# One transformer-style layer on one core: bias tables, masks, attention stacks and the program's head moved to other places

## The chip, the core and the metric

The kernel runs on one core of a Trainium2 chip. The metric is device microseconds of one execution, of which the median over several runs is taken. A profile of one execution comes with it. Engine names are those of the profile: PE is TensorE (PEld its weight loads), DVE is VectorE, ACT is ScalarE, POOL is GpSimd, SP is SyncE, which here only issues transfers.

## The reference

One layer over x of 1024 tokens by 1024 features, float32, with a norm before and after each of three parts:

```
h = swiglu(rmsnorm(x, g)) ; x = x + 0.5 * rmsnorm(h, g')           # FFN 1, width 2816
q, k, v = rmsnorm(x, g) @ w_qkv                                     # 16 heads of 64
o_na  = neighbourhood attention of heads 0-7 on a 16 x 64 grid of tokens,
        window 8 x 16, with a learned bias per (row, column) offset
o_dil = heads 8-15: windows (128,1), (512,4), (2048,16), T5 bias, merged by softmax weights
x = x + rmsnorm([norm(o_na) | norm(o_dil)] @ w_out, g)
h = swiglu(rmsnorm(x, g)) ; x = x + 0.5 * rmsnorm(h, g')           # FFN 2
```

## The kernel before

Every float32 product is three matmuls of split operands (`mm3`: hi*hi, hi*lo, lo*hi); ACT makes the high part with a cast and DVE the low part with a subtraction. The FFNs and the value and q/k projections run as products of halves in a Strassen-like scheme of seven passes per 2 x 2 blocks (`PASSES`).

The program is a chain of stages. PE's order is written by hand throughout (`ordered`); in the first lines of the program that of DVE and ACT too. Elsewhere a planner orders the other engines by its own costs; `c.behind(f, ENGINE)` puts what `f` issues behind the last instruction that the engine was given so far, and `queued` does so for SP and POOL, whose queues issue the transfers. `plan(n, {turn: [...]})` and `c.todo` hang side work on turns of a stage, one turn at each `c.tick()`.

1. The head (`begin` in `layer`): x is loaded, the first norm is computed with a square root on ACT (`rstd_by_sqrt`), the gain's row is spread over the partitions by a matmul (`spread_gain`, tile `gps`), the first three gate weights are split.
2. FFN 1. `PairGemm.ahead` makes two of the seven gate and up products for the first nine column blocks; `PairGemm.run` makes the rest in 22 turns ("gated products"); `Passes.run` then multiplies by the down weights ("down stage"). Sums of down weights (`RightSums`) ride on turns of the gated products, those of value weights on turns of the down stage.
3. Values and q/k: two value passes (`vp.run(0, 1)`), the early half of q/k (`pg.ahead`), value passes 2 to 6, then `pg.run`. Value passes take weights from rotating tiles `pw` (pool `pr`) and raw ones `praw` (pool `pw`).
4. Beside value passes 4 and 5 `build_bias` makes two kinds of tables in DRAM: `gab`, for each dilated head 128 rows that each hold the same 511 numbers shifted by one (two transfers, one per dilation), and `nb`, for each neighbourhood head a 128 x 384 table that is first filled with -1e30 and then gets 16 groups of rows from `stk`. All are issued on POOL's queue.
5. Attention, a head at a time, dilated pairs first. `load_head` loads a stack `st` (q twice and both parts of k twice, 128 x 3 x 1024) in four transfers on POOL's queue, values (`va`, `vb` or `vs`) and the bias on SP's. POOL reorders q and bias of the next dilated head, or adds the mask `cmask` to the next neighbourhood bias (line 1557). Results `ob` of the strided part are brought into token order as `obn` by 16 transfers on SP (`regroup`), merged by POOL's two products and DVE's addition (`merge`), and normed (`GroupNorm`). `nat_fillers` makes matmuls of the output projection that `c.fill` puts between units of neighbourhood heads.
6. The output projection, then FFN 2 like FFN 1.

Of the kernel before, what the change touches and what calls it, by code (L numbers as in the profile page):

```python
# [10 lines left out]
F32 = mybir.dt.float32  # L11
# [231 lines left out]
def rstd_by_sqrt(c, ss):  # L243

    nc, k = c.nc, ss.shape[1]
    h, y, e = [c.small.tile([P, 4], F32, tag=t, name=t)[:, :k] for t in ("v", "y", "e")]
    nc.vector.tensor_add(h, ss[:, :, 0], ss[:, :, 1])
    nc.vector.tensor_scalar(h, h, 1.0 / D, EPS, op0=ALU.mult, op1=ALU.add)
    nc.scalar.activation(e, h, AF.Sqrt)
    nc.vector.reciprocal(y, e)  # L250
    nc.vector.tensor_mul(e, y, h)
    nc.vector.tensor_mul(e, e, y)
    nc.vector.tensor_scalar(e, e, -0.5, 1.5, op0=ALU.mult, op1=ALU.add)
    nc.vector.tensor_mul(y, e, y)
    return y


def spread_gain(c, g, tag, row, one):
# [4 lines left out]
    nc.gpsimd.dma_start(row, g)  # L263
# [44 lines left out]
def nat_fillers(c, x, part, halves):  # L308


    for g in halves:
        ws = []
        for t in range(4):
            acc = []
            for k in range(4):
                def filler(g=g, t=t, k=k, ws=ws, acc=acc):
                    ws.extend(() if ws else nat_weights(c))
                    acc.extend(() if acc else [nat_bank(c)])
                    nat_mm(c, acc[0], x, t, k, ws, True, True)
                    if k == 3:  # L320
                        c.nc.scalar.copy(part[:, t, g * T:(g + 1) * T], acc[0])
# [31 lines left out]
class PairGemm:  # L353
# [4 lines left out]
    def __init__(self, c, op, srcs, early, sink):  # L358
        self.c, self.op, self.srcs, self.early, self.sink = c, op, srcs, early, sink
        self.n, self.raw, self.w, self.kept = len(srcs), {}, {}, {}  # L360
# [242 lines left out]
class Passes:  # L603
# [4 lines left out]
    def __init__(self, c, n, left, right, take, last=None):  # L608
# [4 lines left out]
        if self.own:  # L613
            self.groups[0] = [groups[0][:2], groups[0][2:]] + groups[1:]
# [3 lines left out]
    def fetch(self, w=None, raws=()):  # L618
# [4 lines left out]
        if w is None:  # L623
            w = c.pr.tile([P, 1 + self.own, 2, 2, T], F32R, tag="w", name="pw")
            w = [w[:, side] for side in range(1 + self.own)]
        for side in range(1 + self.own):
# [6 lines left out]
            hi, lo = [w[side][:, h, :m] for h in range(2)]  # L633
            nc.scalar.copy(hi, raw[:, :m])  # L634
            nc.vector.tensor_sub(lo, raw[:, :m], hi.bitcast(F32))  # L635
        for j, i in enumerate(ids):
            lhs = [w[0][:, h, j, :] for h in range(2)] if self.own else [h[:, i, :] for h in self.left.x[a]]
            self.ready.append((lhs, [w[-1][:, h, j, :] for h in range(2)]))
# [134 lines left out]
def build_bias(c, rel, t5, onehot, lncount):  # L773
# [4 lines left out]
    t5t = c.bp.tile([32, 8], F32, tag="b0", name="t5t")  # L778
    nc.gpsimd.dma_start(t5t, t5.rearrange("h b -> b h"))
    for i in range(2):  # L780
        oh = c.bp.tile([P, T], F32, tag="oh", name="oh")
        cols = slice(511 * i, 511 * i + 511)
        nc.gpsimd.dma_start(oh[:32, :511], onehot[:, cols])
        lc = c.bp.tile([P, T], F32, tag="lc", name="lc")
        nc.gpsimd.dma_start(lc[:8, :511], lncount[:, cols].broadcast_to([8, 511]))
        ps = c.pst.tile([P, 4, P], F32, tag="tr", name="tabp").rearrange("p a b -> p (a b)")
        nc.tensor.matmul(ps[:8, :511], t5t, oh[:32, :511], start=True, stop=True)
        nc.vector.tensor_add(lc[:8, :511], ps[:8, :511], lc[:8, :511])
        nc.gpsimd.dma_start(tab[i, :, :511], lc[:8, :511])
        g = c.gab[i]  # L790
        dst = bass.AP(tensor=g.tensor, offset=g.offset, ap=[[P * 640, 8], [641, P], [1, 511]])
        nc.gpsimd.dma_start(dst, tab[i, :, :511].unsqueeze(1).broadcast_to([8, P, 511]))
    neg = c.bp.tile([P, T], F32, tag="oh", name="neg")
    nc.gpsimd.memset(neg[:, :384], NEG)
    nc.gpsimd.dma_start(c.nb.rearrange("h p r e -> p h (r e)"), neg[:, :384].unsqueeze(1).broadcast_to([P, 8, 384]))
    for cc in range(8):
        nc.gpsimd.dma_start(stk[cc], rel[:, :, 7 - cc:31 - cc])
    for r in range(16):
        r0 = min(max(r - 4, 0), 8)
        nc.gpsimd.dma_start(c.nb[:, r * 8:r * 8 + 8, r0:r0 + 8, :].rearrange("h c r e -> c h (r e)"),  # L800
                            stk[:, :, r0 - r + 7:r0 - r + 15, :].rearrange("c h r e -> c h (r e)"))

# [52 lines left out]
def load_stack(c, p, hd):  # L855

    nc = c.nc
    st = c.stk.tile([P, 3, SEQ], F32R, tag="st", name="st")
# [38 lines left out]
class DilPair:  # L897
# [78 lines left out]
    def outs(self, hd, part, quad, un, pt, po):  # L976
# [14 lines left out]
        if (hd, part, quad) == (1, 1, 1):  # L991
            self.regroup()
# [4 lines left out]
    def regroup(self):  # L997

        c, nc = self.c, self.c.nc
        self.obn = c.op.tile([P, 8, RW], F32, tag="obn", name="obn")  # L1000
        for ci in range(4):
# [37 lines left out]
def na_v(c, p):  # L1039
    vs = c.vp[0].tile([P, 8, P], F32, tag="v" + "ab"[p % 2], name="vs")  # L1040
    src = c.v[0][:, p * P:(p + 1) * P].rearrange("(r s c) f -> r c s f", r=16, s=8)
    for r in range(16):
        c.nc.sync.dma_start(vs[r * 8:r * 8 + 8], src[r])
# [97 lines left out]
def layer(tc, a, out):  # L1141
    nc = tc.nc
    c = Ctx(tc)
    with ExitStack() as ctx:
# [22 lines left out]
        c.ob = [c.dr.tile([SEQ, RW], F32, name=f"ob{g}") for g in range(4)]  # L1167
# [35 lines left out]
        def one_a_turn(steps, n, first):  # L1203
            plan(n, {first + i: [f] for i, f in enumerate(steps)})

# [10 lines left out]
        def early_pools(stack, n=3):  # L1216
            c.wr, c.sp = pool("wr", 3, stack), pool("sp", n, stack)
# [7 lines left out]
        def ffn(which, op, prep, pg, get, turns, sums, more, post, pre, src, dst, begin=None):  # L1225
# [24 lines left out]
            one_a_turn(sums, NF, NF - 3 - len(sums))  # L1250
            prep2, ps = sub(), []

            def final():
# [9 lines left out]
                ps[0].fetch([w0[:, i] for i in range(2)], raws[:2])  # L1263
                ps[0].fetch([w.rearrange("p (h j) x -> p h j x", h=2) for w in w1], raws[2:])
# [15 lines left out]
            spread(more, 36)  # L1280
# [408 lines left out]
```

## Time and profile before

| | |
|---|---|
| runs | 1956.1 us median of 3 (1954.6 to 1963.72) |
| profiled execution | 1954.35 us |
| its span, first to last instruction | 1952.6 us |
| granted TensorE clock, mean | 0.985 |
| busy: PE, PEld | 1870.2, 1557.4 us |
| busy: DVE, ACT, POOL | 1330.1, 808.5, 327.5 us |
| moved by DMA | 398.11 MB, 204 GB/s over the span |

Matmuls are pipelined, so that busy time of PE is time in which at least one was under way. Idle time of PE in a stage is the window's length less PE's busy time. In a timeline row stand start and length in us, engine, line, operation, what it writes and reads, and in brackets how long the engine sat idle before it and what ended that. A wait for several things is put down to the one that came last by the profile.

### The profile page before, as it was taken

The page shows a single profiled execution, that of the slowest core. Times are in us where ns is not written, and L with a number is a line of the kernel's source. Part 1 is how long each engine was busy: PE and PEld are TensorE (multiplying, and loading weights), DVE is VectorE, ACT ScalarE, POOL GpSimd, SP SyncE. Part 2 cuts the span into 40 slices and gives each one's busy share as a digit, 9 for nine tenths or more (in the row PEclk, how much of TensorE's full clock was granted, in tenths as well). Part 3 has the DMA queues.
Part 4 walks back from the last instruction along what each step waited for, and adds up shares of the span by engine and source line. Part 5 has one row for each costly group of instructions (what it writes and reads, how often), then busy time and mean ns, then how long its engine had stood idle before and what let it go on. Part 6 is the DMA issues. An engine that isn't in the chain of part 4 may idle for free.

```text
span 1952.6 us, 25603 instructions
## 1 busy us (share of the span) xinstructions
PE 1870.2 (96%) x9048; PEld 1557.4 (80%) x9048; DVE 1330.1 (68%) x2234; ACT 808.5 (41%) x1471; POOL 327.5 (17%) x526
## 2 busy tenths in 40 slices
PE   6999999999999999999999788998999999999997
PEld 5788888888888778778898777877888888888886
DVE  6877876775656775477665565676788777755567
ACT  5522333334534554133676555454222333344333
POOL 2101111111000123423434220021011111110000
PEclk9999999999999999999999899999999999999999
DMA  6645566547876668758999981475456665476563
GB/s 228 227 159 192 187 220 225 186 166 268 305 251 204 228 236 281 228 183 242 222 190 157 159 153 49 139 277 189 167 180 202 234 224 190 155 267 219 199 229 138
DMA packets 170322, 398.11 MB, mean 204 GB/s; under 512 B 20097, under 2 KB 41521, under 8 KB 170193
## 3 DMA queue, kind: packets, MB, share of 16 engines
q1 hardware_dynamic: 118800, 222.34, 36.2%
q0 software_dynamic: 50528, 172.03, 27.9%
q10 hardware_dynamic: 864, 2.10, 0.3%
q8 instruction: 71, 1.16, 0.3%
q14 instruction: 59, 0.48, 0.1%
HBM read 272.03 MB, written 127.26 MB: 204 GB/s over the span
## 4 chain that ended last, share of the span: by engine, by line
PE 79%; DMA 7%; DVE 6%; issue 4%; ACT 2%; SPq 1%; POOL 1%; DVEq 0%; POOLq 0%; ACTq 0%
PE mmp L281 16%; PE mmp L283 16%; PE mmp L282 15%; PE accp L281 8%; PE accp L282 8%; PE accp L283 8%; PE po L985 2%; PE ptp L891 1%; PE po L1085 1%; PE trp L159 1%; DMA va<-v 1%; DMA obn<-ob 1%; DMA wraw<-in_wqk_dram 1%; PE sp L965 1%; DMA x<-x 1%
## 5 line engine op out<-in xcount | busy, mean ns | idle before, releaser
L281 PE MATMUL mmp<-x,whi 128*128 128x512 f32 (+1 forms) x1464 | 580.9, 397 | 8.8 <-ACT whi L374 3.5
L283 PE MATMUL mmp<-x,wlo 128*128 128x512 f32 (+1 forms) x1464 | 575.2, 393 | 2.3 <-DVE wlo L375 2.3
L282 PE MATMUL mmp<-x,whi 128*128 128x512 f32 (+1 forms) x1464 | 574.9, 393 | 0.7 <-DVE x L161 0.6
L281 PEld LDWEIGHTS mmp<-x,whi 128*128 128x128 f32 x1464 | 278.3, 190 | 69.0 <-ACT whi L374 4.2
L283 PEld LDWEIGHTS mmp<-x,wlo 128*128 128x128 f32 x1464 | 278.1, 190 | 64.5 <-DVE wlo L375 3.8
L282 PEld LDWEIGHTS mmp<-x,whi 128*128 128x128 f32 x1464 | 278.4, 190 | 59.2 <-DVE x L161 1.5
L635 DVE TENSOR_TENSOR pw<-praw,pw 128x1024 fp32r<-128x1024 f32 (+1 forms) x182 | 199.2, 1138 | 122.8 <-ACT pw L634 122.5
L634 ACT CAST pw<-praw 128x1024 fp32r<-128x1024 f32 (+1 forms) x182 | 169.0, 983 | 208.8 <-PE accp L283 163.8
L374 ACT CAST whi<-wraw 128x1024 fp32r<-128x1024 f32 x129 | 135.1, 1050 | 252.2 <-PE mmp L282 214.5
L281 PE MATMUL accp<-pw 128*128 128x512 f32 x600 | 234.2, 390 | 0.0
L283 PE MATMUL accp<-pw 128*128 128x512 f32 x600 | 233.5, 389 | 0.0
L282 PE MATMUL accp<-pw 128*128 128x512 f32 x600 | 233.4, 389 | 0.0
L375 DVE TENSOR_TENSOR wlo<-wraw,whi 128x1024 fp32r<-128x1024 f32 x129 | 157.6, 1224 | 23.2 <-ACT whi L374 23.0
L283 PEld LDWEIGHTS accp<-pw 128*128 128x128 f32 x600 | 112.6, 188 | 23.7
L282 PEld LDWEIGHTS accp<-pw 128*128 128x128 f32 x600 | 112.7, 188 | 23.3
L281 PEld LDWEIGHTS accp<-pw 128*128 128x128 f32 x600 | 112.6, 188 | 22.8
L581 POOL DMA_DIRECT2D g<-sg x44 | 23.8, 540 | 470.8 <-DVE sg L574 302.7
L535 DVE TENSOR_TENSOR c<-mmp,u 128x512 f32<-128x512 f32 x52 | 35.9, 691 | 83.9 <-PE mmp L283 83.8
L393 ACT COPY s<-mmp 128x512 f32<-128x512 f32 x52 | 30.5, 587 | 145.9 <-PE mmp L283 140.8
L374 ACT CAST whi<-traw 128x512 fp32r<-128x512 f32 x52 | 32.3, 621 | 117.0 <-PE mmp L282 54.8
L462 DVE TENSOR_TENSOR wraw<-wraw 128x1024 f32<-128x1024 f32 x52 | 63.6, 1224 | 23.3 <-DMA wraw<-in_wqk_dram 14.2
L161 DVE TENSOR_TENSOR x<-trp,x 128x512 fp32r<-128x512 f32 x84 | 57.3, 687 | 31.0 <-ACT x L160 30.9
(258 smaller groups left out, 2793.4 us busy)
## 6 DMA issues: line engine op xcount, KB each, us to landing
praw<-g SPq DMA_DIRECT2D x70, 512.0 KB
wraw<-in_wg_dram SPq DMA_DIRECT2D x44, 512.0 KB
wraw<-in_wu_dram SPq DMA_DIRECT2D x44, 512.0 KB
tr<-in_wd_dram SPq DMA_DIRECT2D x44, 512.0 KB
g<-sg POOLq DMA_DIRECT2D x88, 256.0 KB, 3.9
ts<-tr POOLq DMA_DIRECT2D x22, 1024.0 KB, 4.7
praw<-ts SPq DMA_DIRECT2D x88, 256.0 KB
praw<-in_wd_dram SPq DMA_DIRECT2D x66, 256.0 KB
```

Of the source, the lines that this page charges most:

```text
L161: nc.vector.tensor_sub(lo, ps, hi.bitcast(F32))
L281: nc.tensor.matmul(out, ahi, bhi, start=start, stop=False, skip_group_check=go_on)
L282: nc.tensor.matmul(out, ahi, blo, start=False, stop=False, skip_group_check=go_on)
L283: nc.tensor.matmul(out, alo, bhi, start=False, stop=stop, skip_group_check=go_on)
L374: nc.scalar.copy(hi, raw)
L375: nc.vector.tensor_sub(lo, raw, hi.bitcast(F32))
L393: self.c.nc.scalar.copy(s, ps)
L462: nc.vector.tensor_sub(r[:, 0:2], r[:, 1:3], r[:, 0:2])
L535: nc.vector.tensor_add(c21, d, u2)
L634: nc.scalar.copy(hi, raw[:, :m])
L635: nc.vector.tensor_sub(lo, raw[:, :m], hi.bitcast(F32))
L985: nc.tensor.matmul(po[:, un * 2 + j], pt[:, 2 * j + t, :], rhs, start=t == 0, stop=t == 1)
```

## The change

- Tables: `build_bias` becomes `bias_steps`. Its steps are hung on turns 1 to 8 of FFN 1's gated products; each `gab` table is written as four transfers of 32 rows for all eight heads, the fill as two, each step behind the last instruction of POOL.
- Masks: the eight masked neighbourhood tables are made on POOL in the down stage of FFN 1 and stored as `nm`; a head loads both tables from DRAM.
- Stacks: one half (64 partitions) is loaded on POOL's queue and one on SP's; up to head 8 each third stack has a tile of its own, and the loads of a stack and of the rest of a head are separate steps.
- Value slices `vs` of a pair come in 8 transfers of 16 strided partitions instead of 16 of 8; `obn` is fetched in two groups of 8, each after its quad.
- Norms of the dilated half: the steps of the two groups are placed apart, the output projection's weights are fetched earlier, its fillers come as two products each.
- Values and q/k: the first pass starts on two terms; its first tile, and every third early q/k weight, have the pool `p0`; other rotating tiles are one fewer (`pr`, `wr`).
- The head: the gain's row is loaded first, on SP; x tiles 0 and 1 come as halves on SP and ACT; the third weight is fetched at once; the root has one operation less behind it and the order of ACT and DVE is another; one subtraction moves from POOL to DVE.

The diff, cut to its core:

```diff
@@ rstd_by_sqrt, spread_gain
-    nc.vector.tensor_scalar(h, h, 1.0 / D, EPS, op0=ALU.mult, op1=ALU.add)
-    nc.scalar.activation(e, h, AF.Sqrt)
+    nc.vector.tensor_scalar(h, h, 0.5 / D, 0.5 * EPS, op0=ALU.mult, op1=ALU.add)
+    nc.scalar.activation(e, h, AF.Sqrt, scale=2.0)
+    yield
     nc.vector.reciprocal(y, e)
-    nc.vector.tensor_mul(e, y, h)
+    nc.vector.scalar_tensor_tensor(e, y, -1.0, h, op0=ALU.mult, op1=ALU.mult)
     nc.vector.tensor_mul(e, e, y)
-    nc.vector.tensor_scalar(e, e, -0.5, 1.5, op0=ALU.mult, op1=ALU.add)
-    nc.vector.tensor_mul(y, e, y)
+    nc.vector.scalar_tensor_tensor(y, e, 1.5, y, op0=ALU.add, op1=ALU.mult)
...
-    nc.gpsimd.dma_start(row, g)
+    nc.sync.dma_start(row, g)
@@ nat_fillers
-            for k in range(4):
+            for k in (0, 2):
...
-                    nat_mm(c, acc[0], x, t, k, ws, True, True)
-                    if k == 3:
+                    for i in (k, k + 1):
+                        nat_mm(c, acc[0], x, t, i, ws, True, True)
+                    if k:
@@ PairGemm.split_left, Passes.__init__
-            self.w[b] = self.split(self.raw.pop(b), "g")
+            self.w[b] = self.split(self.raw.pop(b), "g", self.own if b % 3 == 0 else None)
...
-        if self.own:
-            self.groups[0] = [groups[0][:2], groups[0][2:]] + groups[1:]
+        self.groups[0] = [groups[0][:2], groups[0][2:]] + groups[1:]
@@ bias_steps (replaces build_bias)
+    def step(turn, f, *args):
+        at.setdefault(turn, []).append(lambda: c.behind(lambda: f(*args), POOL))
...
+    def toeplitz(i, q):
+        g, n = c.gab[i], P // 4
+        dst = bass.AP(tensor=g.tensor, offset=g.offset + q * n * 641, ap=[[641, n], [P * 640, 8], [1, 511]])
+        nc.gpsimd.dma_start(dst, tab[i, :, :511].unsqueeze(0).broadcast_to([n, 8, 511]))
...
+    def masked(h):
+        if h == 0:
+            got["mask"] = c.bp.tile([P, 384], F32, tag="m", name="mask")
+            nc.gpsimd.dma_start(got["mask"], cmask)
+        if h:
+            t = got.pop(h - 1)
+            nc.gpsimd.tensor_add(t, t, got["mask"])
+            nc.gpsimd.dma_start(c.nm[h - 1], t)
+        if h < 8:
+            got[h] = tile("lc" if h % 2 else "oh", 384)
+            nc.gpsimd.dma_start(got[h], c.nb[h].rearrange("p r e -> p (r e)"))
+    for i in range(2):
+        step(2 + 2 * i, load, i)
+        step(4 + 2 * i, table, i)
+        for q in range(4):
+            step(5 + 2 * i + q // 2, toeplitz, i, q)
+    for cc in range(8):
+        step(1 + cc // 4, stack, cc)
+    step(2, clear, 0)
+    step(3, clear, 4)
+    for r in range(16):
+        step(4 + r // 4, rows, r)
+    return at, [lambda h=h: c.behind(lambda: masked(h), POOL) for h in range(9)]
@@ load_stack, regroup, na_v, na_bias
-    for u in range(2):
-        dst = slice(u * 64, u * 64 + 64)
-        nc.gpsimd.dma_start(st[dst, 0, :], q[u, rows, :])
-        nc.gpsimd.dma_start(st[dst, 1:3, :], k[:, rows, :].rearrange("j p n -> p j n"))
+    for u, queue in enumerate((nc.gpsimd, nc.sync)):
+        to = st[u * 64:u * 64 + 64].bitcast(F32)
+        queue.dma_start(to[:, 0, :], q[u, rows, :])
+        queue.dma_start(to[:, 1:3, :], k[:, rows, :].rearrange("j p n -> p j n"))
...
-        if (hd, part, quad) == (1, 1, 1):
-            self.regroup()
+        if hd and part:
+            self.regroup(quad)
...
-    for r in range(16):
-        c.nc.sync.dma_start(vs[r * 8:r * 8 + 8], src[r])
+    for ci in range(8):
+        c.nc.sync.dma_start(vs[ci:P:8], src[ci])
...
+    c.nc.sync.dma_start(nb[:, 1], c.nm[2 * p + hd])
@@ layer: ffn
-            one_a_turn(sums, NF, NF - 3 - len(sums))
+            if tables:
+                c.bp = pool("bp", 1, w)
+            for i, f in enumerate(sums):
+                tables.setdefault(NF - 3 - len(sums) + i, []).append(f)
+            plan(NF, tables)
...
-            spread(more, 36)
+            spread(more + masks, 36)
@@ layer: loading of heads
+                own = i < 9 and i % 3 == 2
+                stacks.append(load_stack(c, *heads[i], c.op if own else c.stk, 1 if own else 2))
...
-        def next_head():
-            if len(loaded) < 2:
-                load_head()
+        def next_head(i):
+            if i != 9:
+                load_st()
+            if i:
+                load_rest()
             return loaded.popleft()
@@ layer: begin (order of the head)
+            op0.gain, *gains = spread_gain(c, a["ffn1_pre_g"], "pre", xn[0][:1], xn[1][:1, :P])
+            for t in range(2):
+                for h, q in enumerate((nc.sync, nc.scalar)):
+                    q.dma_start(xs[t][:, half[h]], x0[t][:, half[h]])
...
+                w2 = c.xp.tile([P, D], F32, tag="xn", name="w2", bufs=c.xn)
+                pg.raw[2] = w2.rearrange("p (i x) -> p i x", i=2)
+                nc.sync.dma_start(w2, pg.srcs[2][0])
...
                 square(0)
+                gains[0]()
                 square(1, 0)
-                square_dve(1, 1)
-                op0.gain, gain0, gain1 = spread_gain(c, a["ffn1_pre_g"], "pre", xn[0][:1], xn[1][:1, :P])
-                gain0()
-                r = [rstd_by_sqrt(c, ss[0])]
+                square(1, 1, xn[1][:, half[1]])
+                root = rstd_by_sqrt(c, ss[0])
+                next(root)
...
                 hi0(0)
-                lo0(0, nc.gpsimd)
-                gain1()
-                scaled(r, 0, 0, 1)
+                gains[1]()
                 square(2)
+                r0 = next(root)
+                scaled(r0, 0, 0, 1)
+                lo0(0)
@@ layer: values and q/k
-            c.pr, c.pw, c.vt = pool("pr", 3, e), pool("pw", 2, e), pool("vt", 2, e)
+            c.pr, c.pw, c.vt = pool("pr", 2, e), pool("pw", 2, e), pool("vt", 2, e)
...
-            plan(8, {0: [lambda: fin.scale(4, 4), A(4, 5)], 4: [U(4)], 5: [lambda: queued(pg.start)]})
+            p0 = pg.own = pool("p0", 1, prep, side="right")
+            vp.fetch([[p0.tile([P, 2, T], F32R, tag="g" + h, name="pw0" + h) for h in ("hi", "lo")]])
+            plan(12, {0: [lambda: fin.scale(4, 4), A(4, 5)], 8: [U(4)], 9: [lambda: queued(pg.start)],
+                      11: [lambda: pg.split_left(0)]})
             vp.run(0, 1, upto=1)
             e.close()
-            early_pools(e, 2)
+            early_pools(e, 2, 2)
...
-            c.behind(lambda: build_bias(c, a["na_rel_bias"], a["t5_rel_bias"], a["onehot"], a["lncount"]), POOL)
@@ layer: attention
-            c.todo.extend([lambda: (queued(c.w.fetch), squares[0]()), squares[1], scales[0],
-                           lambda: (scales[1](), queued(c.w.fetch))]
-                          + puts[:4] + [begin] + puts[4:])
+            c.todo.extend([squares[0], scales[0]] + puts[:4] + [begin, squares[1], lambda: None, scales[1]])
+            for f in puts[4:]:
+                c.todo.extend([lambda: None, f])
...
-            load_head()
...
-                    else:
-                        nc.gpsimd.tensor_add(g[:, 1], g[:, 0], c.cmask)
...
+                    if (p, hd) == (2 * NP - 1, 1):
+                        queued(lambda: [c.w.fetch() for _ in range(2)])
```

More of the change, by code (lines that the diff above doesn't have):

```diff
@@ L1223, in gate_pairs, with ffn @@
             return PairGemm(c, op, [(wg[f], wu[f]) for f in range(NF)], early, GatePairs(c, which))
-        def ffn(which, op, prep, pg, get, turns, sums, more, post, pre, src, dst, begin=None):
+        def ffn(which, op, prep, pg, get, turns, sums, more, post, pre, src, dst, begin=None, tables=()):
             w = sub()
@@ L1402, in begin @@
                 hi1(0)
+                square(3, 0)
+                square(3, 1, junk()[:, half[1]])
+                root = rstd_by_sqrt(c, ss[1])
+                next(root)
                 lo1(0)
-                square(3, 0)
-                square_dve(3, 1)
-                for hi, lo in ((hi0, lo0), (hi1, lo1)):
-                    hi(1)
-                    lo(1, nc.gpsimd)
+                hi0(1)
+                hi1(1)
+                hi2(0)
                 acc, s1 = [pg.bank() for _ in range(3)], []
```

161 lines of the change are left out of this document (85 added, 76 removed).

## The prediction

> **What bounds the kernel now.** I read the page first: the span, the busy table and the chain.
>
> ```profile
> span 1952.6 us, 25603 instructions
> PE 1870.2 (96%) x9048; PEld 1557.4 (80%) x9048; DVE 1330.1 (68%) x2234; ACT 808.5 (41%) x1471; POOL 327.5 (17%) x526
> PE 79%; DMA 7%; DVE 6%; issue 4%; ACT 2%; SPq 1%; POOL 1%; DVEq 0%; POOLq 0%; ACTq 0%
> ```
>
> TensorE is the bound, busy 1870.2 of 1952.6. No matmul of the large products is removed, so a gain can only come from the 82.4 us in which PE is idle and from half-speed clock behind such pauses. Next, therefore, the view by windows, cut at the places of the change (columns: window, length, busy us of PE, PEld, DVE, ACT, POOL, granted clock, DMA share, GB/s).
>
> ```profile
> 0.00:85.00 85.00, 67.96 (x332) 53.88 (x333) 60.26 (x112) 44.66 (x78) 19.90 (x40) 0.98 0.66 229
> 85.00:675.00 590.00, 590.00 (x2602) 485.33 (x2601) 417.46 (x529) 215.77 (x291) 63.72 (x112) 1.00 0.62 218
> 675.00:715.00 40.00, 35.59 (x146) 26.99 (x145) 29.97 (x56) 19.68 (x33) 8.87 (x17) 0.91 0.66 235
> 795.00:845.00 50.00, 44.54 (x181) 35.54 (x180) 19.97 (x27) 6.83 (x8) 18.26 (x31) 0.93 0.72 214
> 935.00:1060.00 125.00, 116.23 (x977) 114.03 (x976) 81.33 (x331) 90.94 (x301) 52.12 (x58) 0.97 0.99 192
> 1085.00:1145.00 60.00, 43.94 (x284) 40.04 (x283) 39.07 (x125) 33.66 (x106) 15.41 (x19) 0.83 0.91 161
> 1145.00:1220.00 75.00, 67.49 (x443) 59.23 (x442) 41.28 (x127) 39.70 (x120) 7.18 (x12) 1.00 0.44 82
> ```
>
> PE idle by stage is length less busy: head 17.0, start of values and q/k 4.4, end of values 5.5, dilated attention 8.8, first neighbourhood heads 16.1, last heads 7.5: 59.3 us, in exactly the stages that the change edits. Clock lost on top is length times (1 - clock): 3.6, 3.5, 3.8 and 10.2 us from the third row on (without 1145, where it is 1.00), at most, since an idle PE loses nothing by it. Between 85 and 675 PE never stops, and two parts of the change go there: they can cost, not gain.
>
> **The change part by part.**
>
> Head. From the timeline:
>
> ```profile
> 5.65 1.06 ACT L151 ACTIVATE junk<-x 128x1024 f32<-128x1024 f32 x1 [2.49 <-DMA x<-in_x_dram]
> 7.88 3.75 PE L268 MATMUL gps<-xn 1*128 1x512 f32 x4 [7.88 <-DMA xn<-in_ffn_pre_g_dram]
> 10.44 0.21 ACT L249 ACTIVATE e<-v 128x2 f32<-128x2 f32 x1
> 11.24 1.26 POOL L1380 TENSOR_TENSOR wlo<-graw,whi 128x512 fp32r<-128x512 f32 x1 [8.99 <-ACT whi L1377]
> 11.27 1.25 DVE L253 TENSOR_SCALAR e<-e 128x2 f32<-128x2 f32 x1
> 12.82 1.41 DVE L1364 SCALAR_TENSOR_TENSOR xn<-x,y,gain 128x512 f32<-128x512 f32 x2
> ```
>
> The gain row lands at 7.88, the root waits on ACT for the gain's copy until 10.44, and a 128x2 operation of DVE takes 1.25 us while POOL subtracts beside it; so the first scaling starts at 12.82. After, the row goes out first on SP, ahead of x; x as halves on the same two queues lands no sooner than 5.65. Then a square (1.06) and, each at about half of it, the gain's copy and half a square make the sums known at about 7.8, then come two small operations, the root (0.21) and four more, one less than before, none beside POOL, at some 0.2: scaling at about 9.2. That is 3.6 earlier. The third weight tile is now fetched here as well, 512 KB among x2 and x3 on SP; bound 0 to 5, taken 3.5.
>
> Start of values, and of q/k:
>
> ```profile
> L635 DVE TENSOR_TENSOR pw<-praw,pw 128x1024 fp32r<-128x1024 f32 (+1 forms) x182 | 199.2, 1138 | 122.8 <-ACT pw L634 122.5
> L634 ACT CAST pw<-praw 128x1024 fp32r<-128x1024 f32 (+1 forms) x182 | 169.0, 983 | 208.8 <-PE accp L283 163.8
> 708.80 0.50 PE L281 MATMUL mmp<-x,whi 128*128 128x512 f32 x1 [1.66 <-ACT whi L374]
> ```
>
> The first q/k weight is split only when the pools of the value pass have closed; with a tile of its own (p0) it is split in the last turn before. 1.66 goes, and some of the 4.4 less 1.66 = 2.7 us of other idle (the value pass starts on two terms instead of four, from a prefetched tile). Against it: two rotating value tiles instead of three, so the fourth fetch waits for the end of the first pass, and a cast and a subtraction (0.98 and 1.14 on the mean) stand before its use, with six matmuls of 0.227 (590.00/2602 in the window of 85:675), 1.4 us, as cover: about 0.8 us. Taken 3.0 with 1.2 of clock; bound -1 to 6.
>
> Tables. They leave the end of the value passes:
>
> ```profile
> 801.77 0.50 PE L282 MATMUL accp<-pw,x 128*128 128x512 f32 x1 [2.85 <-DVE pw L635]
> 796.36 2.32 POOL L792 DMA_DIRECT2D gab<-tab  x2 [1.00 <-DMA tab<-lc]
> 816.44 0.56 POOL L800 DMA_DIRECT2D nb<-stk  x1 [14.43 <-DMA gab<-tab]
> 823.07 1.69 POOL L1471 DMA_DIRECT2D v<-ha  x3
> 823.87 15.53 SPq L496 DMA_DIRECT2D s<-s1d  x4
> 829.22 0.69 DVE L500 TENSOR_TENSOR u<-mmp,s 128x512 f32<-128x512 f32 x1 [4.65 <-DMA s<-s1d]
> 840.31 0.50 PE L281 MATMUL mmp<-x,whi 128*128 128x512 f32 x1 [1.99 <-DVE c L527]
> gab<-tab POOLq DMA_DIRECT2D x2, 2044.0 KB, 20.3
> ```
>
> POOL's queue stands 14.43 us behind two table transfers of 20.3; the value rows go out only at 823, the kept product is loaded at 823.87, and DVE and PE wait. The 5.5 idle and up to 3.5 of clock go; what releases SP at 823.87 isn't named, so 7.5 taken, bound 0 to 9.0. In the gated products the same bytes come as eight quarters and small copies, over eight turns of five products of twelve matmuls, 0.227 each: 13.6 us a turn. Cover: DMA share 0.62, and PE 590.00 of 590. Queued behind each wait on POOL stand the g and kept-product stores, needed turns later. Cost taken 0, bound by what the same tables cost at their old place: 9.0.
>
> The Trainium skill (DMA: Bandwidth & Descriptors, "Rules for kernel authors") says that an outermost dimension of fewer than 16 confines a transfer to that many engines; before, it is 8 heads, after 32 rows. By it a quarter would take an estimated 20.3/4/2 = 2.5 us instead of 5.1 by bytes; no run here shows it yet, and the sum doesn't use it.
>
> Masks. In the down stage eight loads, additions and stores, and the value sums move closer together (14 steps in 36 turns). PE is full there, but the start is thin:
>
> ```profile
> 470.00:500.00 30.00, 30.00 (x134) 24.81 (x133) 19.88 (x19) 14.22 (x17) 2.21 (x4) 1.00 0.97 343
> 479.55 1.05 ACT L634 CAST pw<-praw 128x1024 fp32r<-128x1024 f32 x1 [7.88 <-DMA praw<-in_wd_dram]
> ```
>
> ACT waits 7.88 for a weight and PE does not notice. A value sum can't start before the last one's tile is stored, so DMA adds little; next late would be that cast. Taken 0, bound -7.9.
>
> Attention:
>
> ```profile
> 943.01 1.06 PE L965 MATMUL sp<-st 128*128 128x256 f32 x4 [3.40 <-DVE sa L881]
> 1035.15 1.22 DVE L1035 TENSOR_TENSOR og<-oa,obn 128x1024 f32<-128x1024 f32 x1 [2.28 <-POOL obn L1031]
> 996.80 11.09 SPq L1003 DMA_DIRECT2D obn<-ob  x16
> 983.35 11.11 SPq L914 DMA_DIRECT2D va<-v  x12
> st<-qk POOLq DMA_DIRECT2D x32, 512.0 KB, 9.3
> 1078.35 1.01 POOL L1557 TENSOR_TENSOR nb<-nb,cmask 128x384 f32<-128x384 f32 x1 [13.29 <-DMA nb<-nb]
> 1093.16 0.77 PE L1069 MATMUL sp<-st 128*128 128x256 f32 x2 [5.66 <-DMA st<-qk]
> 1107.74 1.65 PE L1085 MATMUL po<-vs,pt 128*128 128x128 f32 x6 [2.96 <-ACT pt L893]
> L1115 ACT ACTIVATE junk<-og 128x256 bf16<-128x256 f32 x16 | 6.4, 402 | 0.0
> L1122 DVE SCALAR_TENSOR_TENSOR og<-og,y,gd 128x512 f32<-128x512 f32 x8 | 6.2, 838 | 0.0
> PE accp L281 <- ACT hs L321: 3.4, 4, 1.0
> ```
>
> (a) Start: the pair loads of the second pair move behind the first head; the 3.40 is DVE and ACT finishing q/k, which stays. 1.0; bound -2 to 4. (b) Merges: DVE waits 2.28 for POOL's products; POOL issues two stack transfers less a head and obn starts a quad earlier. 1.5; bound -4 to 6. (c) 1093.16: POOL stands 13.29 behind a late bias to add the mask, the stack is queued behind, and PE waits 5.66. The addition is gone and stacks load two heads ahead (one from the tenth on), so at least a head of 125/8 = 16 us against a landing of 9.3. 5.66 and 2.3 of clock: 8.0; bound 3 to 9. Next late would be the value slices, halved from 16 to 8 transfers. (d) Norms: 16 squares (6.4) in a row on ACT, eight scalings (6.2) on DVE, by the groups of 1085 to 1145. They now come as two groups apart; a group still blocks. Of the 16.1 idle less 5.66, and the clock, 4.0; bound 0 to 15. (e) Pairs as fillers leave the bank three units of rest: 2.0 of 3.4; bound -2 to 3.4. (f) SP gets two more stack transfers and a mask load a head: -2.5 for new waits; bound -10 to 0.
>
> Sum: 3.5 + 3.0 + 7.5 + 1.0 + 1.5 + 8.0 + 4.0 + 2.0 - 2.5 = 28.0. The profiled execution took 1954.35 (1.75 outside the span), the median shown is 1956.1; 1954.35 - 28.0 = 1926.4, and at the median's distance 1928.
>
> The Trainium skill and the trace differ on the clock. In 675:715 the longest pause quoted is 1.66 and the clock is 0.91. Its page TensorE: Matmul & The Clock Gate, "Part 1", lets the clock fall after an idle window of some 3.4 us; by that the short pauses of values and tables would give back no clock, and the sum would be an estimated 1.2 + 2.0 lower, 1931. The measured clock decides; I keep 1928.
>
> **The rivals.**
>
> No gain in attention: the stalls go, and SP's queue makes new ones. For it, 996.80 and 983.35: of the 31 us of a pair (125/4) SP spends 22 on two groups. Against it, loads two heads ahead. Then (a) to (e), 16.5, vanish and (f) reaches 8: 1928 + 16.5 + 5.5 = 1950.
>
> Collision in the gated products: a table quarter delays weights until PE waits. Against it, share 0.62. Costs 9.0: 1937.
>
> The change doesn't do what it says for the tables: SP's load at 823.87 waits for something else and PE stalls as before. 1928 + 4 = 1932, still inside the forecast's own range.
>
> Slower: the stack's half on SP is queued behind obn transfers that wait for PE's own results, so each of seven dilated heads waits as 1093.16 does, 5.66 and 1.7 of clock (half of the 3.6 lost in 675:715). It decides once SP needs more than 31 us a pair: now obn 11.1, va 11.1 and eight of vb and g at obn's 0.69 each, 27.7; four stack halves more, 30.5, by the dearest price. 1928 + 7 x 7.4 = 1980.
>
> Better: all attention stalls go, (d) at 12, (b) at 6, (f) at 0, head 5: 1928 - 16.5 = 1911, and 1905 with 6 more of the 10.2 of clock.
>
> **How the numbers follow.** Forecast 0.60 (own range 1912 to 1943), no gain in attention 0.15, collision 0.10, slower 0.08, better 0.07. Half a per cent of 1956, 9.8 us, is about what can be told from no change here; faster is below 1946.3: 0.60 + 0.10 + 0.07 = 0.77; same 0.15; slower 0.08. Range 1905 to 1950: outside remain the slower case, half of the no-gain case and a little of the better one.
>
> **What would show it.** Head: first scaling near 9 instead of 12.82. Tables: no 2.85 and no 1.99 between 795 and 845, clock 1.00 there; PE still without idle between 85 and 675. Stacks: no wait of sp for st near 1090. Norms: PE idle in 1085:1145 down from 16.1 to some 6. Wrong it would be if PE waits for praw or wraw in the first two stages, or for st, va or obn behind SP.

## The result, and the profile after

| | before | after |
|---|---|---|
| median of 6 runs each | 1957.04 us (1954.60 to 1963.72) | 1946.55 us (1941.23 to 1949.89) |
| ratio of the runs, 95% interval | | 0.9936 (0.9913 to 0.9959) |
| profiled execution: span | 1952.6 us | 1944.7 us |

The change gains 10.5 us where 28 were forecast. The page of the changed kernel (busy table, chain):

```profile
PE 1865.8 (96%) x9048; PEld 1551.8 (80%) x9048; DVE 1328.4 (68%) x2233; ACT 810.1 (42%) x1471; POOL 323.5 (17%) x517
PE 66%; DMA 13%; issue 9%; DVE 7%; ACT 2%; POOL 1%; SPq 1%; DVEq 0%; POOLq 0%; ACTq 0%
```

TensorE idles 78.9 us instead of 82.4, and transfers now carry 13% of the chain instead of 7%. The same windows as in the prediction say where (window, length, busy us of PE, PEld, DVE, ACT, POOL, granted clock, DMA share, GB/s):

```profile
0.00:85.00 85.00, 68.24 (x336) 53.50 (x337) 58.12 (x109) 45.74 (x79) 18.17 (x38) 0.98 0.59 208
85.00:675.00 590.00, 579.29 (x2518) 470.51 (x2517) 410.29 (x514) 211.74 (x283) 106.19 (x176) 1.00 0.67 233
675.00:715.00 40.00, 38.40 (x179) 30.95 (x179) 30.79 (x62) 16.82 (x30) 6.73 (x13) 1.00 0.56 198
795.00:845.00 50.00, 48.45 (x213) 39.48 (x212) 27.52 (x36) 8.32 (x9) 6.53 (x12) 1.00 0.38 137
1085.00:1145.00 60.00, 49.21 (x345) 44.38 (x344) 36.98 (x127) 37.40 (x119) 8.21 (x10) 0.93 0.77 180
```

Idle fell from 5.5 to 1.6 in 795:845 and from 16.1 to 10.8 in 1085:1145, but 85:675, where PE never stopped, now holds 10.7 us. A window at a fixed time shifts against the work, however. A surer reading takes the start of the same matmul in both kernels: first of the down stage, of the value pass, of attention, of the second gated stage. From the timeline of before, then of after:

```profile
464.36 0.39 PE L281 MATMUL accp<-pw 128*128 128x512 f32 x1
678.26 0.50 PE L281 MATMUL accp<-pw,x 128*128 128x512 f32 x1 [0.50 <-ACT pw L634]
937.94 0.28 PE L965 MATMUL sp<-st 128*128 128x256 f32 x1
1287.54 0.50 PE L281 MATMUL mmp<-x,whi 128*128 128x512 f32 x1 [1.82 <-ACT whi L374]
```

```profile
475.06 0.39 PE L281 MATMUL accp<-pw 128*128 128x512 f32 x1
695.85 0.39 PE L281 MATMUL accp<-pw0hi,x 128*128 128x512 f32 x1
941.72 0.28 PE L1009 MATMUL sp<-st 128*128 128x256 f32 x1
1281.35 0.50 PE L281 MATMUL mmp<-x,whi 128*128 128x512 f32 x1 [1.82 <-ACT whi L375]
```

Differences of neighbouring rows are the lengths of the stages (us; the last two columns are kernels of the experiments below):

| stage | before | after | tables put back | three edits |
|---|---|---|---|---|
| head and gated products | 464.4 | 475.1 | 464.9 | 467.0 |
| down stage | 213.9 | 220.8 | 214.6 | 215.9 |
| values, q/k | 259.7 | 245.9 | 253.1 | 245.1 |
| attention, output projection | 349.6 | 339.6 | 329.9 | 330.8 |
| rest of the span | 665.1 | 663.4 | 667.8 | 664.1 |

Each length is from one profiled execution. So the change earned 13.8 + 10.0 us from the values on and lost 10.7 + 6.9 in the first feed-forward. A finer mark splits the first row: ACT's first cast of a `wraw` tile, at 91.26 us before, 90.47 after, 90.42 with the tables put back and 90.23 with three edits. From there to the down stage it is 373.1, 384.6, 374.5 and 376.7 us. By this mark the new head was worth only 0.8 us in the changed kernel, and the gated products lost 11.5. Which waits are new, the view of waits of PE says (waited for: us, times, longest):

```profile
PE accp L282 <- DVE pw L636: 7.0, 6, 2.1
PE accp L281 <- ACT hs L322: 5.5, 1, 5.5
PE mmp L281 <- DVE c L529: 5.0, 2, 3.0
```

The 5.66 for the stack is gone. New are the 5.0 in the gated products, most of the 7.0 (splits of down weights), and 5.5 where the fillers begin.

### The profile page after: what moved, and what is told of

The parts are those of the page before. It is cut to its first block, busy times and chain, and to the rows that moved or that the text cites. A ratio compares the mean times of both kernels' runs of the same rounds, so it can differ in the third digit from the quotient of the medians.

```text
span 1944.7 us, 25641 instructions
## 1 busy us (share of the span) xinstructions
PE 1865.8 (96%) x9048; PEld 1551.8 (80%) x9048; DVE 1328.4 (68%) x2233; ACT 810.1 (42%) x1471; POOL 323.5 (17%) x517
## 4 chain that ended last, share of the span: by engine, by line
PE 66%; DMA 13%; issue 9%; DVE 7%; ACT 2%; POOL 1%; SPq 1%; DVEq 0%; POOLq 0%; ACTq 0%
PE mmp L283 13%; PE mmp L281 13%; PE mmp L282 13%; PE accp L282 7%; PE accp L281 7%; PE accp L283 7%; PE po L1029 2%; DMA wraw<-in_wu_dram 2%; DMA tr<-in_wd_dram 2%; PE trp L159 1%; PE ptp L935 1%; DMA tsv<-tr 1%; PE sp L1009 1%; PE po L1131 1%; DMA st<-qk 1%
## 5 line engine op out<-in xcount | busy, mean ns | idle before, releaser
L394 ACT COPY s<-mmp 128x512 f32<-128x512 f32 x52 | 30.5, 587 | 134.8 <-PE mmp L283 129.6
```

Source lines behind the costliest of these rows:

```text
L394: self.c.nc.scalar.copy(s, ps)
```

## The experiments

Each is named with its ratio to the kernel before on the same chip, with the 95% interval. A cost or gain in us is the difference of two ratios times 1957 us; medians from different chips are not compared, since the kernel before took 1958.38, 1958.07 and 1955.83 us on the three chips used.

**Are the moved tables the loss?** The tables are built in one piece behind the value passes again, and POOL adds the mask again (summary of the edit):

```
-  bias_steps(...) in ffn 1; nb[:, 1] <- c.nm by SP
+  c.behind(lambda: build_bias(...), POOL) after vp.run(2, 3)
+  nc.gpsimd.tensor_add(g[:, 1], g[:, 0], c.cmask)
```

> The changed kernel with the tables and masks where they were: the tables built in one piece behind the value passes, the mask added by POOL in attention; everything else of the change stays. Theory A: the tables and masks are what slowed the first feed-forward. The same matmul runs 11.5 us later from the end of the head to the start of the down stage, and 7.6 us more by its end; both go (19), and the value stage loses again what it had gained there, 3.9 us of idle time and about 3.5 of clock, so 1946.5 - 19 + 8 = about 1936; the down stage starts near 464 instead of 475.1. Rival: the delay comes from the head's new order, which shifts all later transfers; then the down stage still starts near 475 and the time is 1946.5 + 8 = about 1954.

Measured: 1931.03 us, 0.9863 (0.9842 to 0.9884), 14.3 us faster than the changed kernel. Its rows:

```profile
464.90 0.39 PE L281 MATMUL accp<-pw 128*128 128x512 f32 x1
679.48 0.39 PE L281 MATMUL accp<-pw0hi,x 128*128 128x512 f32 x1
932.60 0.28 PE L1037 MATMUL sp<-st 128*128 128x256 f32 x1
1262.53 0.50 PE L281 MATMUL mmp<-x,whi 128*128 128x512 f32 x1 [1.82 <-ACT whi L375]
```

With the new head in place, nearly all of the loss in the first feed-forward goes: from the mark to the down stage it is 374.5 us instead of 384.6 (with the new head alone, an experiment below, 374.3), and the down stage takes 214.6 instead of 220.8 (before, 213.9). So the tables and masks caused it, not the head. The values lose 253.1 - 245.9 = 7.2 us again, and attention is 9.7 us better, which theory A had not said; the third question below answers that.

**What in the tables costs?** First thinner transfers, the same in number and size:

```
-  step(5 + 2 * i + q // 2, toeplitz, i, q);  step(4 + r // 4, rows, r)
+  step(5 + 8 * i + 2 * q, toeplitz, i, q);   step(4 + r, rows, r)
```

> The changed kernel with the same table transfers spread thinner over the gated products: one quarter every second turn from turn 5 to 19 instead of two a turn from 5 to 8, one row block a turn from 4 to 19 instead of four a turn. Theory A1: two quarters and four row blocks together keep the DMA queues full for about 8 us, so that the weights issued beside them land after 7 to 10 us instead of 4 to 6; singly they fit: the waits at 204 and 299 go, the down stage starts near 468 instead of 475.1, about 1940. Rival A2: not the amount at a time but any table work on POOL's queue delays the stores of the down sums behind it and with them DVE; then more turns carry it and the loss stays or grows: 1946 to 1952.

Measured: 1937.74 us, 0.9896 (0.9875 to 0.9917): 7.8 us back. The mechanism is in the changed kernel's timeline:

```profile
193.47 1.21 POOL L806 DMA_DIRECT2D gab<-tab  x2
195.21 2.31 POOL L820 DMA_DIRECT2D nb<-stk  x4
204.02 1.04 ACT L375 CAST whi<-wraw 128x1024 fp32r<-128x1024 f32 x1 [5.33 <-DMA wraw<-in_wg_dram]
206.98 0.50 PE L281 MATMUL mmp<-x,whi 128*128 128x512 f32 x1 [2.96 <-DVE c L529]
```

Two quarters and four row blocks go out on POOL's queue; the weight that SP issues behind them at 196.93 lands after 7.1 us (the median of the gate weights in 85 to 480 is 4.0 with the tables put back); ACT waits 5.33 for it, and PE 2.96 for what DVE does after that. Issue rows for 85 to 480 (KB each, median us to landing), changed kernel and then the thin one:

```profile
gab<-tab POOLq DMA_DIRECT2D x8, 511.0 KB, 7.4
```

```profile
gab<-tab POOLq DMA_DIRECT2D x8, 511.0 KB, 4.1
```

The share of the DMA engines in 85 to 480 is 0.60 with the bunched transfers and 0.62 with the thin ones: the mean does not show the difference. The traces of the other runs repeat it: from the mark to the down stage four kernels with bunched tables take 381.9 to 384.7 us, and seven with thin ones 376.4 to 377.3. That is still some 2 us more than the 374.5 without tables there.

Next the other half: value sums at turns 7, 14, 21, 28 and 35 again, with the masks between:

```
-  spread(more + masks, 36)
+  spread(more, 36), and mask step i in turn 2 + 4 * i
```

> The changed kernel with the value sums of the down stage again at turns 7, 14, 21, 28 and 35, and the nine mask steps in turns 2, 6, 10 and so on between them. Theory B: DVE waits 18.3 us for value tiles that its order puts ahead of the splits of the down weights, because the five steps stand at turns 2 to 12; apart, these waits fall to some 7 as before, the 4.7 us of PE idle between 510 and 570 go and with them most of the 7.6 us: about 1940. Rival: the masks' own transfers, or the later start of the stage, make the weights late; then the idle time stays and the time is 1946.

Measured: 1940.25 us, 0.9912 (0.9888 to 0.9935): 4.7 us back. DVE's waits between 85 and 675 separate the two causes. For the tiles of the value sums (wv) and of the down sums (wd), the changed kernel, the thin one, the one with the sums apart, and the one with both edits:

```profile
DVE tr L347 <- DMA tr<-in_wv_dram: 18.3, 4, 7.8
DVE tr L347 <- DMA tr<-in_wd_dram: 16.0, 5, 4.6
```

```profile
DVE tr L347 <- DMA tr<-in_wv_dram: 20.6, 4, 7.7
DVE tr L347 <- DMA tr<-in_wd_dram: 1.1, 1, 1.1
```

```profile
DVE tr L347 <- DMA tr<-in_wd_dram: 16.3, 5, 4.4
DVE tr L347 <- DMA tr<-in_wv_dram: 9.1, 1, 9.1
```

```profile
DVE tr L350 <- DMA tr<-in_wv_dram: 8.9, 1, 8.9
DVE tr L350 <- DMA tr<-in_wd_dram: 1.1, 1, 1.1
```

Each edit takes away its own wait and leaves the other; for the value sums what remains, 9.1, is near the 6.8 of the kernel before. DVE took its instructions in the order given: a sum whose tile has not landed holds up the splits that PE needs. In the down stage most of the loss goes with the closer turns: four kernels with the close turns take 219.8 to 221.2 us there, seven with the sums apart 215.2 to 218.0, against 213.9 before. Whether the masks' bytes make up the rest was not tried. Rows and quarters of the tables were thinned together and are not separated.

**Where did attention's gain go?** The first two output weights are split some turns before the fillers begin:

```
-  c.todo.extend([squares[0], scales[0]] + ...
+  c.todo.extend([lambda: (squares[0](), c.w.split()), scales[0]] + ...
```

> The changed kernel, with the first two weights of the output projection split a few turns before the fillers begin, so that the loads of the next two stand ahead of the next neighbourhood heads' loads in SP's queue instead of behind them. Theory D: the 5.5 us that TensorE waits at 1136.6 come from SP. The third and fourth weight are issued at 1125.5, behind a stack half and the loads of tables and masks; ACT's cast waits for the third, the copy that frees the fillers' only bank stands behind that cast. So the wait goes, with up to 3.4 us of half clock: 1946.5 - 7 = about 1939. Rival: the bank's copy is late because ACT does the eight squares of the second norm group there; then the wait stays and the time is 1946.

Measured: 1937.33 us, 0.9901 (0.9885 to 0.9917): 6.8 us back, and the wait of 5.5 is gone from the view of waits. In the changed kernel the chain reads, from the timelines of SP, ACT (two rows) and PE:

```profile
1125.54 0.94 SPq L106 DMA_DIRECT2D wraw<-in_wo_dram  x2
1136.74 1.04 ACT L116 CAST whi<-wraw 128x1024 fp32r<-128x1024 f32 x1 [4.10 <-DMA wraw<-in_wo_dram]
1141.48 0.56 ACT L322 COPY hs<-accp 128x512 f32<-128x512 f32 x1
1142.10 0.80 PE L281 MATMUL accp<-whi,o 128*128 128x512 f32 x1 [5.49 <-ACT hs L322]
```

SP reached the third and fourth weight only at 1125.5, behind a stack half, tables and masks; the copy `hs` stood in ACT's queue behind the cast of the third. Between cast and copy ACT also does the eight squares that the rival named, from 1137.69 to 1140.8, so they were part of the delay. They were not enough for it by themselves: the edit leaves them where they were, and the wait is gone. That is term (f). It also answers the first question: with POOL adding the masks again, SP has fewer loads and issues the two weights at 1101.93 instead of 1125.54, and the wait is absent there too.

**Are the three separate?** All three edits in one kernel:

> The changed kernel with the three edits together: table transfers one quarter every second turn, value sums at their old turns with the masks between, and the output weights split earlier. If the three causes are separate, their gains add: 8.8 (thin tables, 1946.55 - 1937.74), 6.3 (value sums apart, 1946.55 - 1940.25) and 7 (weights) give 1946.5 - 22 = about 1924, below the 1931 of the kernel whose tables stayed behind the value passes. Rival: the tables' bytes still cost the first feed-forward what they save in the value stage; then it ends no lower than 1931.

Measured: 1925.45 us (1924.66 to 1926.29), 0.9838 (0.9823 to 0.9853). It gives back 19.2; the single ones add up to 7.8 + 4.7 + 6.8 = 19.3, closer than their intervals, some 4 us to either side, would let one expect. Singly, their intervals overlap that of the changed kernel, and the waits and the stage lengths had to tell them apart; together they are clear of it. The kernel is clear of the one before, too. Against the kernel with the tables put back the intervals just overlap, but the stages speak against the rival: the moved tables cost 2.1 + 1.3 us in the first feed-forward and save 8.0 in the values. Its rows:

```profile
466.95 0.39 PE L284 MATMUL accp<-pw 128*128 128x512 f32 x1
682.88 0.39 PE L284 MATMUL accp<-pw0hi,x 128*128 128x512 f32 x1
927.99 0.28 PE L1012 MATMUL sp<-st 128*128 128x256 f32 x1
1258.77 0.50 PE L284 MATMUL mmp<-x,whi 128*128 128x512 f32 x1 [1.82 <-ACT whi L378]
```

**Were the gains sized right?** The head on the kernel before, alone (the edit is the head's part of the diff):

> The kernel before with the new head alone: gain row first on SP, x in halves, the shorter root, the third weight tile from its own fetch. Theory C: the first products start 3 to 5 us earlier and nearly all of it is lost again where TensorE then waits for the tiles 4 and 5 of x, whose own chain (load, squares, root, scaling) moved only 1.4 us: 1957.0 - 1 = 1956. Rival, the term of the prediction: 1957.0 - 3.5 = 1953.5.

Measured: 1954.23 us, 0.9985 (0.9971 to 0.9999): 2.9 us, closer to the term of 3.5 than to theory C, with an interval that takes in both. By the mark the head is 3.4 us earlier here (87.82 instead of 91.26), so in this trace theory C's loss did not occur. In the kernels with the whole change the mark lies anywhere between 88.3 and 91.8, one trace each; why the same head gains less there was not taken apart.

The other parts were undone on the kernel with the three edits. The start of values and q/k:

```
-  p0 = pg.own = pool("p0", ...); vp.fetch([[p0.tile(...) ...]]); plan(12, ...)
+  plan(8, {..., 4: [U(4)], 5: [lambda: queued(pg.start)]}), value tiles three deep
```

> The kernel with the three edits together, and the start of values and of q/k as before the change: no weight tile of its own, no prefetched value tile, first value terms four at a time, three rotating value tiles. The prediction's term was 3.0 with clock: 1925.5 + 3 = 1928.5. Theory F: the same matmul gained 5.0 us from the end of the down stage to the end of the q/k start in the kernel with the tables put back (from 1.9 late to 3.1 early), so the term was too small and this gives about 1930.5. Rival: those 5 us come from the later tables, not from the start: 1925 to 1926.

Measured: 1928.76 us, 0.9866 (0.9843 to 0.9889): worth 5.5 us by the ratios; the intervals overlap. In the traces the stretch from the down stage to attention is 464.8 us long, against 460.4 to 462.4 in the five other kernels that keep the three edits and the new start, 3.7 above their mean. Both the term and theory F fit, the rival less.

Stacks on one queue, first on the changed kernel:

```
-  for u, queue in enumerate((nc.gpsimd, nc.sync)):
+  for u, queue in enumerate((nc.gpsimd, nc.gpsimd)):
```

> The changed kernel with both halves of each stack on POOL's queue, as before the change; all else as changed. Theory E: what removed the 5.66 us wait for the stack is that POOL no longer stands behind a late table to add the mask and that stacks are asked for two heads ahead; the second queue does little, and SP gets freer: 1943 to 1948. Rival: the two queues are what makes stacks land in time; then TensorE waits for st again near 1090, 5.7 us and the clock, 1952 or more.

Measured: 1951.43 us, 0.9968 (0.9956 to 0.9981), 6.3 us slower. The time is the rival's, but neither mechanism is right: PE does not wait for st, and yet the queue counts. Part of its price was covered, because SP, with fewer loads, came to the output weights at 1092.34 instead of 1125.54 and the fillers' wait went. So again on the kernel without that wait:

> The kernel with the three edits together, and both halves of each stack on POOL's queue. With the changed kernel this cost 4.9 us while the fillers' wait of 5.5 us was gone at once, because SP came earlier to the weights; here that wait is gone already. Theory G: the second queue is worth some 10 us in the dilated heads, not by the stack itself but because POOL's products for the merge stand behind the stack transfers and DVE behind the products: about 1935. Rival: the 4.9 was all: about 1930.

Measured: 1936.52 us, 0.9900 (0.9881 to 0.9918), 12.1 us slower, all of it in attention (342.8 us instead of 330.8). Issue rows and waits, with two queues, then with one:

```profile
st<-qk POOLq DMA_DIRECT2D x10, 512.0 KB, 9.4
st<-qk SPq DMA_DIRECT2D x9, 512.0 KB, 6.9
g<-gab SPq DMA_DIRECT2D x12, 192.0 KB, 4.9
PE po L1032 <- ACT pt L940: 6.6, 4, 2.4
```

```profile
st<-qk POOLq DMA_DIRECT2D x19, 512.0 KB, 9.2
g<-gab SPq DMA_DIRECT2D x12, 192.0 KB, 8.1
DVE s L928 <- DMA g<-gab: 8.9, 2, 7.6
DVE og L1083 <- POOL obn L1079: 5.6, 2, 3.4
ACT whi L120 <- DMA wraw<-in_wo_dram: 5.8, 2, 5.6
PE po L1032 <- ACT pt L940: 11.6, 2, 6.3
PE po L1032 <- DVE pt L940: 6.8, 3, 3.8
```

A POOL half lands no later on one queue (9.2) than on two (9.4), though SP's half had landed in 6.9. The Trainium skill (DMA: Bandwidth & Descriptors, "Rules for kernel authors") says that spreading transfers over queues brings no bandwidth, only issue time; the trace agrees, with 186 GB/s between 930 and 1085 us on two queues and 188 on one. What changed is when other things come. Theory G has the size, but its mechanism only in part: of PE's 11.6 + 6.8 us of waiting for `pt`, the longest two waits stand behind an output weight (6.3; it landed in 11.0 us instead of 7.9) and behind a dilated bias `g` (5.3; SP issued that one only at 961.57, 6.0 us later than with two queues). The merge's products, for which DVE waits 5.6, follow with 3.8 and 2.5. They stood not behind stack transfers but behind POOL's reordering of the next bias and q; the first time POOL had waited 10.5 us for that bias. Why SP's loads are issued or land later when POOL's queue carries both halves was not taken apart.

Fillers as single terms, four to a bank:

```
-  for k in (0, 2):
+  for k in range(4):
```

> The kernel with the three edits together, and the fillers again single terms, four to a bank, instead of pairs, two to a bank. Term (e) of the prediction: pairs save 2.0 of the 3.4 us that TensorE waits for the bank's copy, so this kernel is 2 us slower than the one with pairs, about 1926. Rival: the pairs only move the wait to other places and the two are equal within 1 us.

Measured: 1933.12 us (1925.55 to 1938.10), 0.9874 (0.9854 to 0.9894): pairs are worth 7.0 us with a wide spread, above the 2.0. Attention takes 338.7 us instead of 330.8.

The norms of the dilated half in their old order:

```
+  c.todo.extend([squares[0] (and the split), squares[1], scales[0], scales[1]] + puts[:4] + [begin] + puts[4:])
```

> The kernel with the three edits together, and the two norm groups of the dilated half in the old order: both groups' squares, both scalings, then the transposes. Term (d) of the prediction: 4.0 us with the clock: about 1929.5. Rival: with stacks in time and the weights early the groups only displace each other, 16 squares in a row cost what two groups of eight cost: 1925 to 1926.

Measured: 1931.20 us, 0.9875 (0.9856 to 0.9893): worth 7.2 us, above the 4.0. Attention takes 338.2 us. Part of both figures may be chance: in the kernel with the start undone, whose edit leaves attention alone, that stage took 336.0 us in the profiled execution.

And cut finer than the change does, squares in two turns a group and scalings in four:

```
-  [squares[0], scales[0]] + puts[:4] + [begin, squares[1], lambda: None, scales[1]]
+  [a0, a1, s0, s1, (puts[0], s2), (puts[1], s3), puts[2], puts[3], (begin, b0), b1], the second group alike
```

> The kernel with the three edits together, and the norms of the dilated half cut up: the eight squares of a group in two turns of four, the four scalings in four turns. A group of eight squares holds ACT 3.2 us and TensorE waits 2.7 for the copy behind it; four scalings hold DVE 2.7 us and TensorE waits 2.7 again. Theory H: in pieces both waits fall under 1 us, 4 us with some clock: about 1921. Rival: the pieces stand just as much in the way of the copies, only elsewhere: 1925.

Measured: 1929.37 us, 0.9859 (0.9839 to 0.9880): no gain (the intervals overlap; attention takes 330.9 us against 330.8). PE's wait for `pt` there falls from 3.2 to 1.8, the wait for `og` stays at 2.7, and one of 1.8 for `e` comes in at a later norm.

## Why the prediction was wrong

The direction held, the size did not. By its own steps:

| step | forecast | measured | from |
|---|---|---|---|
| head | 3.5 | 2.9 | head alone on before (0.8 in the changed kernel, by the mark) |
| start of values, q/k | 3.0 | 3.7 to 5.5 | undone: stage lengths, ratios |
| tables out of the value passes | 7.5 | 7.2 | stage lengths |
| tables in the gated products | 0 | -7.8 | thinned (-10.1 in all, by the mark, tables put back) |
| value sums and masks in the down stage | 0 | -4.7 | apart |
| attention, (a) to (e) | 16.5 | 18.8 | stage lengths, three edits |
| of it (d) norms | 4.0 | 7.2 | undone |
| of it (e) pairs as fillers | 2.0 | 7.0 | single |
| (f) new waits behind SP | -2.5 | -6.8 | weights earlier |

The gains were sized well as a whole: without the three costs the change brings 1957 x (1 - 0.9838) = 31.7 us, where the terms without (f) came to 30.5. That they meet so closely is partly luck: by the stages the values gained 14.6 where 10.5 were forecast and attention 18.8 where 16.5 were, while the head fell short and some of the hidden costs remain. Undone one by one, the attention parts are larger than their terms; they share waits, and with one part gone others lengthen. For (c), the stack's own wait is absent in every kernel with the changed attention, with POOL's addition back (tables put back) as with a single queue; one thing that these have in common is that stacks are asked for up to two heads ahead, which was not tried alone. (a) and (b) were not tried by themselves. In the head the first scaling came at 9.78, 3.0 us earlier and not 3.6, and behind it PE waited:

```profile
9.78 1.41 DVE L1436 SCALAR_TENSOR_TENSOR xn<-x,y,gain 128x512 f32<-128x512 f32 x2
40.53 0.94 PE L159 MATMUL trp<-ident,xn 128*128 128x128 f32 x4 [1.95 <-DVE xn L200]
48.24 0.63 PE L159 MATMUL trp<-ident,s 128*128 128x128 f32 x4 [2.27 <-DVE s L223]
```

In this trace the next tiles came little earlier, so PE waited for them: a step that ends sooner is worth only what the next one can follow.

The failed steps are the two zeros, which cost 7.8 and 4.7 us, and (f) in size, 6.8 instead of 2.5. The prediction's own sign of being wrong appeared: PE, without idle between 85 and 675 us before, idled 10.7 us there. The first zero named its cover, a DMA share of 0.62 and a full PE. A mean share says nothing of a burst: two quarters of 7.4 us and four row blocks in one turn are a burst, and the weight that a product needs is issued right behind it. The nearest row had been quoted (20.3 us for a table, POOL 14.43 behind it) and was used as a bound, not as the price. The second zero looked at ACT's cast as the next thing late; it was DVE, behind a sum whose tile is still on its way. The sentence that "a value sum can't start before the last one's tile is stored" was true, and it was just the reason: the sum stood in DVE's order before its tile could be there. (f) named SP's queue but put a flat 2.5 on its new waits, without pricing what stood behind the late load. Each of the three, as the edits give it back, lay inside its own bound (9.0, 7.9, 10), though by the mark the tables' whole cost, 10.1, passed it; that they would come together was in no rival. The collision rival named the mechanism of the first at 9.0 and 0.10. The rival on SP's load at 823.87 was priced at 4 us, where losing the tables' term would have cost 7.5; the prediction does not say why, and the rival did not come. What stays open: with the three edits the down stage still starts 2.6 us later than before, and 4.9 later than with the head alone. Half of that, 2.4, is already there at the mark near 90 us, in the head; the other 2.4 lies in the gated products, where thin tables take 376.7 us against 374.3.

The two sentences on the Trainium skill: by its rule on the outermost dimension (same page and section as above) a quarter would land in an estimated 2.5 us; singly it took 4.1, nearer the 5.1 by bytes. Both estimates start from the 20.3 of two tables in flight together, so this does not settle the rule. On the clock (TensorE: Matmul & The Clock Gate, "Part 1") the trace again sides with the short pauses:

```profile
195.00:215.00 20.00, 16.58 (x65) 12.86 (x64) 14.02 (x19) 5.03 (x6) 6.64 (x13) 0.91 0.62 174
```

The longest wait there is 2.96 us, below the 3.4 that the Trainium skill names, and the clock is 0.91; in 675:715, where the pauses of up to 1.66 went, it rose from 0.91 to 1.00.

## What to carry to other kernels

Work moved beside a full engine is not free because the DMA share is below one: put one large transfer in a turn, not several, and ask what is issued next to it. Before adding an operation to an engine that takes its instructions in the order given, as DVE and ACT did here, see that its data will have landed by then, since everything behind it waits; the same holds for a load on a queue. Where a change has gains and hidden costs of like size, price each "costs nothing" by the nearest row and let the costs come together in one rival.

## What the runs showed of the hardware that was not expected

A table quarter of 511 KB landed in 7.4 us in pairs beside four row blocks and in 4.1 singly beside one, while the mean DMA share was higher with the single ones (0.62 instead of 0.60). Two queues instead of one left the rate of the transfers in the dilated heads as it was (186 and 188 GB/s) and changed the time by 12.1 us; other loads landed sooner with two, the dilated bias in 4.9 us instead of 8.1 and the output weights in 7.9 instead of 11.0. The granted clock was 0.50 between 208 and 211 us of the changed kernel, behind a pause of TensorE of 2.96 us, and 0.52 between 711 and 714 of the kernel before, behind one of 1.66 with shorter ones beside it.
